# The last two column blocks of an attention output projection, split by token halves

## The chip, the cores and the metric

The kernel runs on one core of a Trainium2 chip. The metric is the device time of one execution in microseconds (us), shown as the median of several runs. A profile of one execution gives, for each engine, when every instruction ran and what ended the idle time in front of it: TensorE (PE, with its weight loads PEld), VectorE (DVE), ScalarE (ACT), GpSimd (POOL) and the queue of DMA issues on SyncE (SP).

## The reference

The reference is a two-layer diffusion backbone over 512 latent tokens of width 2048 with a context of 256 tokens. The part around the change is the end of layer 0 and the start of layer 1:

```
y    = concat(y_a, y_b) * silu(gate)              # 512 x 2048
o    = y @ w_out                                  # w_out: 2048 x 2048
x1   = layer_norm(sqrt(2) * x + g_l * o) * g + bias
h    = layer_norm(x1) * (1 + scale) + shift       # layer 1
u, gate = split(h @ w_in, 2)
f    = real(fft2(u per group of 256 columns))
```

The Fourier step over the tokens is done by the kernel as a product with a 512 x 512 matrix (`dft`) ahead of `h @ w_in`.

## The kernel before

Everything is float32; a product is made of three float32r products of high and low parts (`mm3`: hi*hi, lo*hi, hi*lo). `split` makes the two parts of a tile: a cast on ACT (line 41, `hi`) and a subtraction on DVE (line 44, `lo`).

`out_proj` (called by `mixer_out`) computes `y @ w_out`. The 2048 output columns are four blocks of 512 (`n` = 0 to 3). Within a block, the 16 tiles of the contraction (`k`) come in the order of memory: one DMA brings `raw`, two `k` of 128 x 512 (512 KB), each `k` is split into `pgh` and `pgl`, and for each of the four token tiles of 128 (`t` = 0 to 3) three matmuls of 128x128 by 128x512 add it to that token tile's accumulator `oacc` in PSUM. In this text such a split `k` is a page: it costs 12 matmuls for four token tiles and 6 for two. `raw` has 3 buffers, `pgh` and `pgl` have 7. At the end of a block each token tile gets its epilogue on DVE: `tg` = `oacc` times the gate (line 972; `gate` has one buffer, loaded once per block), `xp` = sqrt(2) * `xr` + `tg` (line 976; `xr` is a block of `x`, two buffers), and its sums (line 977).

Block 3 is done in two groups: all 16 `k` for token tiles 0 and 1, then all 16 `k` again for token tiles 2 and 3, with the same weights loaded and split a second time. After the first group `done(1)` runs the two layer norms of token tiles 0 and 1 while TensorE works for tiles 2 and 3: `centre` (line 1034), `power` and `refine` on POOL (lines 1040 to 1047), `affine` (line 1056) for tile 0, and for tile 1 a scale on ACT (line 1137) and one multiplication and one addition per half, the first half on POOL and the second on DVE (lines 1142 and 1143). The results are stored as `x_0` and `x_1` in four DMAs. `late()`, after the second group's weights, and `done(3)`, after its epilogues, bring the rest, among it the first products with `dft` (`contract`). In the last group the last 6 pages are held back (`hold`): tile 2 gets all six first, then tile 3.

```
self.load(self.x1_d[1][:, cs], x[:, cs], True)     # x_1: a store, issued on SP
```

So loads and these stores go out on one queue, SP's, in the order of the program; a DMA that waits for its source or its buffer holds back what stands behind it.

In blocks 0 to 2 a second stream runs on DVE: `tick()` after each page (in block 0 from `k` = 8) takes one 512 KB tile of the modulation weights of layer 1 (`macraw`, three buffers) and adds it to `mac` in two steps (line 197). Forty ticks in all: 8, 16 and 16.

The order of each engine's instructions is made by a scheduler from the program's order and from the readiness that it estimates; calls with `keep_in_program_order` keep theirs.

Of the kernel before, what the change touches and what calls it, by code (L numbers as in the profile page):

```python
# [10 lines left out]
F32 = mybir.dt.float32  # L11
F32R = mybir.dt.float32r
AF = mybir.ActivationFunctionType
ALU = mybir.AluOpType
# [4 lines left out]
ALPHA = math.sqrt(2.0)  # L19
# [5 lines left out]
class Build:  # L25
# [903 lines left out]

    def out_proj(self, w, nk, y, gate_d, res, xp, rawp, pg, tp, acp, st, kq, hold, done, every, late, first=lambda n: None):  # L930
        nc = self.nc
        for n in range(4):
            first(n)
            gt = tp.tile([128, 512], F32, name="gate", bufs=1)
            self.load(gt, gate_d[n])
            acs = [acp.tile([128, 512], F32, name="oacc") for _ in range(4)]
            groups = [(0, 1, 2, 3)] if n < 3 else [(0, 1), (2, 3)]
            for group in groups:
                end = group[-1] == 3 and n == 3
                held = []  # L940
                for q in range(nk // kq):
                    for kk in range(kq):
                        y(kq * q + kk)
                    raw = rawp.tile([128, kq, 512], F32, name="raw")
                    self.load(raw, w(n, q))
                    for kk in range(kq):
                        k = kq * q + kk
                        yh, yl = y(k)
                        hi = pg.tile([128, 512], F32R, name="pgh")
                        lo = pg.tile([128, 512], F32R, name="pgl")  # L950
                        self.split(raw[:, kk, :], hi, lo)
                        if end and k >= nk - hold:
                            held.append((k, hi, lo))
                            continue
                        for t in group:
                            o = 128 * t
                            self.mm3(acs[t], (yh[:, o:o + 128], yl[:, o:o + 128]), (hi, lo), k == 0, k == nk - 1)
                        if every and n < 3 and (n or k >= 8):
                            self.mac_hold = n == 0
                            self.tick()  # L960
                if n == 3 and not end:
                    self.mac_rest()
                if end:
                    late()
                for t in group:
                    o = 128 * t
                    for k, hi, lo in held:
                        self.mm3(acs[t], (y(k)[0][:, o:o + 128], y(k)[1][:, o:o + 128]), (hi, lo), False, k == nk - 1)
                    xr = tp.tile([128, 512], F32, name="xr")
                    self.load(xr, res(t, n))  # L970
                    g = tp.tile([128, 512], F32, name="tg")
                    ins = nc.vector.tensor_mul(out=g, in0=acs[t], in1=gt)
                    if end and t == 3:
                        self.tc.keep_in_program_order(ins)
                    xs = xp[t][:, 512 * n:512 * n + 512]
                    nc.vector.scalar_tensor_tensor(out=xs, in0=xr, scalar=ALPHA, in1=g, op0=ALU.mult, op1=ALU.add)
                    nc.vector.bn_stats(out=st[t][:, n, :], in_=xs)
                    if n == 3:
                        done(t)

    def mixer_out(self, s):
        nc, d = self.nc, self.d
# [719 lines left out]
```

## Time and profile before

| | us |
|---|---|
| median of 3 runs | 2333.34 (2333.04 to 2336.59) |
| the profiled execution | 2323.94, its span 2322.2 |
| TensorE busy | 2147.6 (92% of the span) |
| output projection, first to last matmul | 939.1 to 1143.2 |

The profiled execution lies 9.4 us (0.4%) under the median of the runs. TensorE is busy in most slices of the span; the stretch from the last block of the output projection to the first products of layer 1 is one of those in which it is not.

### The profile page before, as it was taken

How to read it: one execution, taken by the hardware profiler on the slowest of the kernel's cores; microseconds unless marked ns; L12 is line 12 of the kernel's file. 1: busy time of each engine (PE TensorE's matmuls, PEld its weight loads, DVE VectorE, ACT ScalarE, POOL GpSimd, SP SyncE). 2: the span in 40 equal slices, each digit the busy share in tenths (PEclk: the TensorE clock that was granted, in tenths of full speed). 3: DMA queues.
4: the chain of work that ended last, by engine and by line, in shares of the span. 5: the costliest groups of instructions: out<-in, count | busy, mean ns of one | idle time of the engine just before them, and what ended most of it. 6: DMA issues, size and time to landing. Idle time of an engine off the chain costs nothing.

```text
span 2322.2 us, 39267 instructions
## 1 busy us (share of the span) xinstructions
PE 2147.6 (92%) x15708; PEld 1994.3 (86%) x15708; DVE 1886.4 (81%) x2603; ACT 947.0 (41%) x1321; POOL 429.0 (18%) x407
## 2 busy tenths in 40 slices
PE   5999989989999999999788999998999998998994
PEld 3778879889899999777568989998999998998994
DVE  5456799998765588677799998789899899779998
ACT  2222344433444467322463333444343445445331
POOL 1023413100111123000551131002122124002003
PEclk9999999999999999999999999999999999999997
DMA  8852354566511132787427765545455446537333
GB/s 339 310 196 95 124 183 159 188 230 208 208 48 58 60 110 75 229 300 261 169 96 252 273 242 181 182 146 188 156 175 193 150 166 230 174 128 255 117 137 118
DMA packets 128702, 412.63 MB, mean 178 GB/s; under 512 B 14852, under 2 KB 15492, under 8 KB 126728
## 3 DMA queue, kind: packets, MB, share of 16 engines
q1 hardware_dynamic: 113144, 359.04, 45.3%
q0 software_dynamic: 8320, 31.33, 3.8%
q10 hardware_dynamic: 7056, 19.76, 2.2%
q8 instruction: 123, 2.02, 0.4%
q14 instruction: 59, 0.48, 0.1%
HBM read 347.81 MB, written 62.26 MB: 177 GB/s over the span
## 4 chain that ended last, share of the span: by engine, by line
PE 35%; DVE 8%; DMA 3%; issue 3%; ACT 1%; POOL 1%; DVEq 0%; SPq 0%; ACTq 0%; POOLq 0%
PE r L54 33%; DVE wl L44 2%; DMA wraw<-in_wg 2%; PE psd L54 1%; DVE mac L197 1%; DMA stage<-yt 1%; DVE wraw L1185 1%; DVE btl L44 1%; DVE ws L1206 0%; DVE x L1539 0%; DVE c L1219 0%; PE pt L1492 0%; DVE hf L1325 0%; DVE x L1535 0%; POOL btl L44 0%
## 5 line engine op out<-in xcount | busy, mean ns | idle before, releaser
L54 PE MATMUL r<-bth,wl 128*128 128x256 f32 x1848 | 525.1, 284 | 16.8 <-DVE wl L44 16.5
L54 PE MATMUL r<-btl,wh 128*128 128x256 f32 x1848 | 524.6, 284 | 2.3 <-DVE btl L44 1.3
L54 PE MATMUL r<-bth,wh 128*128 128x256 f32 x1848 | 525.2, 284 | 0.2 <-ACT wh L41 0.2
L41 ACT CAST wh<-wraw 128x1024 fp32r<-128x1024 f32 x262 | 274.6, 1050 | 393.1 <-PE r L54 288.0
L44 DVE TENSOR_TENSOR wl<-wraw,wh 128x1024 fp32r<-128x1024 f32 x262 | 335.0, 1283 | 52.3 <-ACT wh L41 52.0
L54 PEld LDWEIGHTS r<-bth,wl 128*128 128x128 f32 x1848 | 351.4, 190 | 19.5 <-DVE wl L44 19.2
L54 PEld LDWEIGHTS r<-btl,wh 128*128 128x128 f32 x1848 | 350.8, 190 | 3.6 <-DVE btl L44 1.7
L54 PEld LDWEIGHTS r<-bth,wh 128*128 128x128 f32 x1848 | 351.8, 190 | 0.9 <-issue 0.5
L41 ACT CAST wh<-ws 128x1024 fp32r<-128x1024 f32 x183 | 191.8, 1049 | 344.3 <-PE r L54 330.4
L44 DVE TENSOR_TENSOR wl<-ws,wh 128x1024 fp32r<-128x1024 f32 x183 | 230.0, 1257 | 12.0 <-ACT wh L41 9.8
L197 DVE SCALAR_TENSOR_TENSOR mac<-macraw,cs,mac 128x512 f32<-128x512 f32 x240 | 193.6, 807 | 11.4 <-DMA macraw<-in_ada 9.9
L54 PE MATMUL r<-hlh,wl 128*128 128x256 f32 (+1 forms) x480 | 147.2, 307 | 26.7 <-DVE wl L44 26.6
L54 PE MATMUL r<-hlh,wh 128*128 128x256 f32 (+1 forms) x480 | 146.3, 305 | 0.6 <-ACT wh L41 0.5
L54 PE MATMUL r<-hll,wh 128*128 128x256 f32 (+1 forms) x480 | 144.9, 302 | 0.0
L54 PE MATMUL r<-bah,wl 128*128 128x256 f32 x384 | 112.7, 293 | 25.1 <-DVE wl L44 25.1
L54 PEld LDWEIGHTS r<-hlh,wl 128*128 128x128 f32 x480 | 93.5, 195 | 33.7 <-DVE wl L44 30.7
L41 ACT CAST pgh<-raw 128x512 fp32r<-128x512 f32 (+2 forms) x104 | 65.7, 662 | 121.8 <-DMA raw<-in_wo 78.2
L54 PE MATMUL r<-bbh,wl 128*128 128x256 f32 x384 | 109.5, 285 | 2.9 <-DVE wl L44 2.9
L54 PE MATMUL r<-bal,wh 128*128 128x256 f32 x384 | 111.2, 290 | 0.0
L54 PE MATMUL oacc<-pgl,yh 128*128 128x512 f32 x256 | 102.1, 399 | 9.7 <-DVE pgl L44 9.7
L54 PE MATMUL r<-bah,wh 128*128 128x256 f32 x384 | 111.1, 289 | 0.0
L54 PE MATMUL r<-bbh,wh 128*128 128x256 f32 x384 | 109.4, 285 | 0.0
(489 smaller groups left out, 5700.1 us busy)
## 6 DMA issues: line engine op xcount, KB each, us to landing
macraw<-in_ada SPq DMA_DIRECT2D x72, 512.0 KB, 6.3
wraw<-in_win SPq DMA_DIRECT2D x66, 512.0 KB, 6.7
raw<-in_adas SPq DMA_DIRECT2D x64, 512.0 KB, 5.1
wraw<-in_wg SPq DMA_DIRECT2D x64, 512.0 KB, 6.6
wraw<-in_wu SPq DMA_DIRECT2D x64, 512.0 KB, 4.3
wraw<-in_wo SPq DMA_DIRECT2D x64, 512.0 KB, 4.7
macraw<-in_ada SPq DMA_DIRECT2D x112, 256.0 KB, 3.9
raw<-in_wo SPq DMA_DIRECT2D x40, 512.0 KB, 5.4
```

Source lines behind the costliest of these rows:

```text
L41: ins = nc.scalar.copy(out=hi, in_=src)
L44: sub = (eng or nc.vector).tensor_sub(out=lo, in0=src, in1=hi.bitcast(F32))
L54: self.pin(self.nc.tensor.matmul(ps, lhsT=a, rhs=b, start=start, stop=stop))
L197: ins = nc.vector.scalar_tensor_tensor(out=acc, in0=raw[:, k, :], scalar=col, in1=acc, op0=ALU.mult, op1=ALU.add)
L1185: nc.vector.tensor_sub(out=raw[1, 0], in0=raw[0, 0], in1=raw[1, 0])
```

## The change

The list of blocks and groups is written out: blocks 0 and 1 for all token tiles, then blocks 2 and 3 for tiles 0 and 1, then blocks 2 and 3 for tiles 2 and 3. In this text the four groups are (2,01), (3,01), (2,23) and (3,23). The weights of block 2 are now loaded and split twice, as those of block 3 were, and the gate of blocks 2 and 3 is loaded for each group. The sixteen ticks of block 2 all stay with its first group. The matmuls are the same in number.

```diff
-        for n in range(4):
-            first(n)
+        every4 = (0, 1, 2, 3)
+        for n, group in ((0, every4), (1, every4), (2, (0, 1)), (3, (0, 1)), (2, (2, 3)), (3, (2, 3))):
+            if group[0] == 0:
+                first(n)
             gt = tp.tile([128, 512], F32, name="gate", bufs=1)
             self.load(gt, gate_d[n])
-            acs = [acp.tile([128, 512], F32, name="oacc") for _ in range(4)]
-            groups = [(0, 1, 2, 3)] if n < 3 else [(0, 1), (2, 3)]
-            for group in groups:
-                end = group[-1] == 3 and n == 3
+            acs = {t: acp.tile([128, 512], F32, name="oacc") for t in group}
+            end = group[-1] == 3 and n == 3
...
-                        if every and n < 3 and (n or k >= 8):
+                    if every and n < 3 and group[0] == 0 and (n or k >= 8):
...
```

The rest of the diff is one level of indentation.

On SP, the queue from the loads of (3,01) on stands so before (`raw`, `gate` and `xr` are loads, `x_0` to `x_3` the stores of the normalized tokens):

```order
L62 DMA gate<-gate_3_97 128x512
L62 DMA xr<-in_x 128x512 x2
L62 DMA raw<-in_wo 128x1024 x8
L62 DMA xr<-in_x 128x512 x2
L62 DMA raw<-in_wo 128x1024 x2
L62 DMA x_0_10166<-xp 128x1024 x2
L62 DMA x_1_10167<-xp 128x1024 x2
L62 DMA x_3_10169<-lngb 128x1024 x2
```

And so from the same place in the changed kernel:

```order
L62 DMA raw<-in_wo 128x1024 x11
L62 DMA gate<-gate_2_96 128x512
L62 DMA xr<-in_x 128x512 x2
L62 DMA raw<-in_wo 128x1024 x2
L62 DMA x_0_10166<-xp 128x1024 x2
L62 DMA x_1_10167<-xp 128x1024 x2
L62 DMA raw<-in_wo 128x1024 x3
L62 DMA gate<-gate_3_97 128x512
L62 DMA xr<-in_x 128x512 x2
L62 DMA raw<-in_wo 128x1024 x5
L62 DMA x_3_10169<-lngb 128x1024 x2
```

Before, no weight load stands behind the four stores; now all eight of (3,23) do (3 and 5).

On DVE, from the last two `pgl` of block 2 to the first of block 3, before:

```order
L44 TENSOR_TENSOR pgl<-raw,pgh 128x512 x2
L197 SCALAR_TENSOR_TENSOR mac<-macraw,cs,mac 128x512 x4
L44 TENSOR_TENSOR pgl<-raw,pgh 128x512 x6
L972 TENSOR_TENSOR tg<-oacc,gate 128x512 x2
L976 SCALAR_TENSOR_TENSOR xp<-xr,tg 128x512 x2
```

And in the changed kernel:

```order
L44 TENSOR_TENSOR pgl<-raw,pgh 128x512 x2
L197 SCALAR_TENSOR_TENSOR mac<-macraw,cs,mac 128x512 x2
L972 TENSOR_TENSOR tg<-oacc,gate 128x512
L197 SCALAR_TENSOR_TENSOR mac<-macraw,cs,mac 128x512
L976 SCALAR_TENSOR_TENSOR xp<-xr,tg 128x512
L197 SCALAR_TENSOR_TENSOR mac<-macraw,cs,mac 128x512
L977 BN_STATS st_10162<-xp 128x6
L972 TENSOR_TENSOR tg<-oacc,gate 128x512
L44 TENSOR_TENSOR pgl<-raw,pgh 128x512
```

The first `tg` (which waits for block 2's last page) now stands ahead of block 3's first `pgl` instead of six behind it.

On DVE at the end of (2,23) in the changed kernel, from the last step of the norm of tile 1:

```order
L1143 TENSOR_TENSOR xp<-xp,lnbb 128x1024
L44 TENSOR_TENSOR pgl<-raw,pgh 128x512 x6
L972 TENSOR_TENSOR tg<-oacc,gate 128x512 x2
L976 SCALAR_TENSOR_TENSOR xp<-xr,tg 128x512 x2
L977 BN_STATS st_10164<-xp 128x6
L977 BN_STATS st_10165<-xp 128x6
L44 TENSOR_TENSOR pgl<-raw,pgh 128x512 x15
```

Of the six `pgl`, five are the last of (2,23) and one is the first of (3,23); the six epilogue instructions of (2,23) stand between (3,23)'s first `pgl` and its other fifteen. Up to this place the order of DVE after (3,01) is as it was before, with four `pgl` where six stand now.

## Rows read from the trace of the kernel before

**Rows 1.** Windows: us, busy PE, PEld, DVE, ACT, POOL, then clock, DMA share, GB/s

```profile
1050.20:1090.00 39.80, 39.79 (x179) 33.05 (x180) 32.41 (x51) 9.14 (x16) 0.00 (x0) 1.00 0.81 270
...
1114.20:1143.20 29.00, 24.07 (x94) 18.14 (x93) 26.50 (x36) 12.82 (x18) 16.36 (x18) 0.94 0.44 153
1143.20:1167.00 23.80, 11.90 (x42) 7.93 (x40) 15.10 (x28) 12.18 (x19) 15.52 (x15) 0.86 0.40 139
```

**Rows 2.** Timeline of PE: start, us, instruction, [idle before, releaser]; 60 matmuls apart

```profile
1054.69 0.39 PE L54 MATMUL oacc<-pgh,yl 128*128 128x512 f32 x1
...
1068.29 0.39 PE L54 MATMUL oacc<-pgh,yl 128*128 128x512 f32 x1
```

**Rows 3.** Lines of DVE by shape in 1049.4 to 1083: count, busy, mean, idle before

```profile
L197 DVE SCALAR_TENSOR_TENSOR mac<-macraw,cs,mac 128x512 f32<-128x512 f32 x25 | 18.7, 750 | 3.9 <-DMA macraw<-in_ada 3.4
L44 DVE TENSOR_TENSOR pgl<-raw,pgh 128x512 fp32r<-128x512 f32 x14 | 9.4, 687 | 2.6 <-ACT pgh L41 2.5
```

**Rows 4.** Timeline of DVE: block 2's last `pgl`, then its first epilogues

```profile
1080.08 1.29 DVE L44 TENSOR_TENSOR pgl<-raw,pgh 128x512 fp32r<-128x512 f32 x2 [0.37 <-ACT pgh L41]
1081.29 3.11 DVE L197 SCALAR_TENSOR_TENSOR mac<-macraw,cs,mac 128x512 f32<-128x512 f32 x4
...
1088.93 1.28 DVE L972 TENSOR_TENSOR tg<-oacc,gate 128x512 f32<-128x512 f32 x2
1090.13 1.28 DVE L976 SCALAR_TENSOR_TENSOR xp<-xr,tg 128x512 f32<-128x512 f32 x2
```

**Rows 5.** Timeline of PE: two waits and the matmuls behind the first

```profile
993.22 1.87 PE L219 MATMUL oacc<-ones,mac 128*128 128x1 f32 x8 [5.05 <-DVE tg L972]
...
995.52 0.63 PE L54 MATMUL oacc<-pgl,yh 128*128 128x512 f32 x1
...
1000.22 0.63 PE L54 MATMUL oacc<-pgh,yh 128*128 128x512 f32 x1
...
1050.21 0.50 PE L54 MATMUL oacc<-pgl,yh 128*128 128x512 f32 x1 [3.19 <-DVE pgl L44]
```

**Rows 6.** Timeline of DVE after (3,01): its first `tg`, the last four `pgl`

```profile
1114.24 0.69 DVE L972 TENSOR_TENSOR tg<-oacc,gate 128x512 f32<-128x512 f32 x1
...
1130.29 6.83 DVE L44 TENSOR_TENSOR pgl<-raw,pgh 128x512 fp32r<-128x512 f32 x4
```

**Rows 7.** Timeline of PE: its last waits of the projection, a slow matmul, the last

```profile
1134.42 0.51 PE L54 MATMUL oacc<-pgl,yh 128*128 128x512 f32 x1 [1.74 <-DVE pgl L44]
...
1137.18 0.70 PE L54 MATMUL oacc<-pgl,yh 128*128 128x512 f32 x1 [1.79 <-DVE pgl L44]
...
1138.54 0.63 PE L54 MATMUL oacc<-pgh,yh 128*128 128x512 f32 x1
...
1142.78 0.39 PE L54 MATMUL oacc<-pgh,yl 128*128 128x512 f32 x1
```

**Rows 8.** Timeline of POOL: the last step of tile 1's first half

```profile
1133.89 2.69 POOL L1143 TENSOR_TENSOR xp<-xp,lnbb 128x1024 f32<-128x1024 f32 x1
```

**Rows 9.** Timeline of SP: the four stores

```profile
1126.33 11.07 SPq L62 DMA_DIRECT2D x<-xp  x4
```

**Rows 10.** Waits of SP in 1040 to 1143: total us, times, longest

```profile
SPq L62 <- POOL xp L1143: 8.7, 1, 8.7
```

**Rows 11.** Tile `raw` in 1040 to 1143: casts, idle ahead of them, landing

```profile
L41 ACT CAST pgh<-raw x46: 602/619/624, 1040.6 to 1131.4; 128x512 fp32r<-128x512 f32 x46
...
  DMA raw<-in_wo: 48.9, 12
...
DMA to landing us min/median/max: 3.5/5.1/7.8
```

**Rows 12.** Timeline of DVE behind the last matmul: token tile 3

```profile
1143.93 1.47 DVE L976 SCALAR_TENSOR_TENSOR xp<-xr,tg 128x512 f32<-128x512 f32 x1
```

**Rows 13.** Timeline of POOL at the same time: token tile 0

```profile
1142.90 1.96 POOL L1087 TENSOR_TENSOR macraw<-xp,macraw 128x768 fp32r<-128x768 f32 x1 [3.08 <-ACT macraw L1086]
```

**Rows 14.** Timeline of ACT behind the projection

```profile
1155.55 1.24 ACT L1076 ACTIVATE xp<-xp,smx 128x1024 f32<-128x1024 f32 x1 [8.41 <-POOL smx L1071]
```

More of the change, by code (lines that the diff above doesn't have):

```diff
@@ L931, in out_proj @@
         nc = self.nc
-        for n in range(4):
-            first(n)
+        every4 = (0, 1, 2, 3)
+        for n, group in ((0, every4), (1, every4), (2, (0, 1)), (3, (0, 1)), (2, (2, 3)), (3, (2, 3))):
+            if group[0] == 0:
+                first(n)
             gt = tp.tile([128, 512], F32, name="gate", bufs=1)
             self.load(gt, gate_d[n])
-            acs = [acp.tile([128, 512], F32, name="oacc") for _ in range(4)]
-            groups = [(0, 1, 2, 3)] if n < 3 else [(0, 1), (2, 3)]
-            for group in groups:
-                end = group[-1] == 3 and n == 3
[L940 to L957, printed above, removed]
-                        if every and n < 3 and (n or k >= 8):
[L959 to L979, printed above, removed]
@@ new lines, in out_proj @@
+            acs = {t: acp.tile([128, 512], F32, name="oacc") for t in group}
+            end = group[-1] == 3 and n == 3
+            held = []
+            for q in range(nk // kq):
+                for kk in range(kq):
+                    y(kq * q + kk)
+                raw = rawp.tile([128, kq, 512], F32, name="raw")
+                self.load(raw, w(n, q))
+                for kk in range(kq):
+                    k = kq * q + kk
+                    yh, yl = y(k)
+                    hi = pg.tile([128, 512], F32R, name="pgh")
+                    lo = pg.tile([128, 512], F32R, name="pgl")
+                    self.split(raw[:, kk, :], hi, lo)
+                    if end and k >= nk - hold:
+                        held.append((k, hi, lo))
+                        continue
+                    for t in group:
+                        o = 128 * t
+                        self.mm3(acs[t], (yh[:, o:o + 128], yl[:, o:o + 128]), (hi, lo), k == 0, k == nk - 1)
+                    if every and n < 3 and group[0] == 0 and (n or k >= 8):
+                        self.mac_hold = n == 0
+                        self.tick()
@@ new lines, in out_proj @@
+            if n == 3 and not end:
+                self.mac_rest()
+            if end:
+                late()
+            for t in group:
+                o = 128 * t
+                for k, hi, lo in held:
+                    self.mm3(acs[t], (y(k)[0][:, o:o + 128], y(k)[1][:, o:o + 128]), (hi, lo), False, k == nk - 1)
+                xr = tp.tile([128, 512], F32, name="xr")
+                self.load(xr, res(t, n))
+                g = tp.tile([128, 512], F32, name="tg")
+                ins = nc.vector.tensor_mul(out=g, in0=acs[t], in1=gt)
+                if end and t == 3:
+                    self.tc.keep_in_program_order(ins)
+                xs = xp[t][:, 512 * n:512 * n + 512]
+                nc.vector.scalar_tensor_tensor(out=xs, in0=xr, scalar=ALPHA, in1=g, op0=ALU.mult, op1=ALU.add)
+                nc.vector.bn_stats(out=st[t][:, n, :], in_=xs)
+                if n == 3:
+                    done(t)
```

## The prediction

> **What bounds the kernel now.** I read the windows first: they tell stage by stage which engine is full. From 1050 to 1090, block 2, TensorE is busy without a break (39.79 of 39.80 us at clock 1.00), but DVE is busy for 32.41 us of it and the DMA engines for 81%: TensorE is the bound with little room beside it. From 1114.2 to 1143.2, the second group of block 3, TensorE loses 5 us and part of its clock, and in the 24 us behind it, where the last norms run, it is busy for half [rows 1]. So a change here can gain in the last two windows and has little slack to spend in the first.
>
> Next the timeline of TensorE, for the price of a page. Sixty matmuls take 1068.29 - 1054.69 = 13.60 us, 0.2267 us each [rows 2]: a page costs 12 x 0.2267 = 2.72 us for four token tiles and 1.36 us for two. A group of two tiles is 16 pages, 21.8 us.
>
> Then DVE in block 2. Fourteen of its sixteen `pgl` and 25 of the tick's additions take 9.4 + 18.7 us in 33 us, and of DVE's 6.5 us of waits 3.4 name `macraw`'s DMA and 2.5 a cast [rows 3], and what ACT waits for ahead of casts is the load of `raw`, 48.9 us in this stretch [rows 11]. Little of that waits for TensorE. Block 2 needs those instructions whether a page feeds 12 matmuls or 6.
>
> Last the queue of SP, whose four stores take from 1126.33 to 1137.40 to be issued [rows 9]; 8.7 us of that is one wait for POOL's last step on tile 1 [rows 10], which ends at 1133.89 + 2.69 = 1136.58 [rows 8]. Today nothing that TensorE needs stands behind these stores.
>
> **The change part by part.** The matmuls stay 768. Added are 16 casts and 16 `pgl`, 8 loads of 512 KB and 2 of a gate. I walk along TensorE's path with the mark M, the start of DVE's first `tg` after (3,01): 1114.24 before [rows 6]. The last matmul then starts at 1142.78 and the group ends at 1143.0 [rows 7], M + 28.8.
>
> *Group (2,01).* DVE's instructions up to block 2's last `pgl` are the same ones in nearly the same order, and so is SP's queue; what they waited for was not TensorE. So that `pgl` again ends at 1080.08 + 1.29 = 1081.4 [rows 4]. But TensorE, which then had 7.5 us of matmuls in hand (to the `tg` at 1088.93), now has only the last two pages, about 10 matmuls from 1080.7 on: it finishes at 1083.0 at full clock, or at 1085.0 at the lower one (0.427 us each, from (1000.22 - 995.52) / 11 in [rows 5]), which its waits in this group may bring. From 1050.21 on [rows 5] it has done 14 pages, 19.0 us, in 33 to 35: some 15 us idle. The first `tg` starts 0.5 to 0.7 us ahead of that end, 1082.5 to 1084.3. Behind it on DVE stand mac, STT, mac, BN, `tg`, and only then block 3's first `pgl`: seven instructions, five at 0.60 (pairs start 1.20 apart) and two at 0.78 (four in 3.11) [rows 4], 4.5 us. TensorE waits about 4 us and goes on at 1087.0 to 1088.8.
>
> *Group (3,01).* 94 matmuls are left, 21.3 us. Its first six pages come from loads issued before the epilogue; the next `raw` follows the second `xr`, about 1.3 us behind that first `pgl`, and with a landing of 5.1 [rows 11], a cast and a `pgl` page 6 is ready 7.6 us behind it, just when it is due (6 x 1.36 less two matmuls is 7.7): no wait, and none to spare. Whether the clock falls in the 4 us wait is open: after 5.05 us of idling it was low for 12 matmuls and more (0.63 long against 0.39), after 3.19 us it was not [rows 5]. A fall costs 13 x 0.2 = 2.6 us; this wait lies between the two, I take half. M comes at 1107.6 to 1112.0, middle 1109.8: **-4.4** (-6.6 to -2.2).
>
> *Group (2,23).* It stands where (3,23) stood, against the same norms of tiles 0 and 1 on DVE, ACT and POOL. The last `pgl` was ready at 1137.18 [rows 7], M + 22.9 (the four `pgl` before it had taken 6.83 us beside POOL [rows 6, 8]); four matmuls later, at M + 23.8, the group ends. The waits of 1.74 and 1.79 us that the change might have spared stay, in this group.
>
> *Group (3,23): the new wait.* Its eight loads stand behind the four stores. The last store is issued at 1137.40, M + 23.2 [rows 9]. A `raw` lands 3.5 to 7.8 us after issue, median 5.1 [rows 11]; the other queues being quiet then (DMA share of the window 0.44 [rows 1]) I take 4.0, bounds 3.5 and 5.1. With 0.6 for the cast [rows 11] TensorE starts at M + 27.8: a wait of **4.0**. The first `pgl` ends at M + 28.4; behind it DVE has six epilogue instructions of (2,23), held there by that `pgl`, 3.6 us at the starts of [rows 4], and then the second `pgl`, ready at M + 32.6. TensorE's first page is done at M + 29.3: a second wait of **3.3**. From there 88 matmuls, 19.95 us, to M + 52.6. The gate and the fourth `raw` follow the epilogues and land about when page 6 is due, so they add nothing I can price. The clock fell before after two waits of 1.74 and 1.79 us close together [rows 7]; with 4.0 and 3.3 I take the fall, 2.6 us. End at **M + 55.2** (52.1 to 56.3), against M + 28.8.
>
> *Behind the projection.* The norms of tiles 2 and 3 start from the last matmuls as before, in the same order on DVE, ACT and POOL; ACT still waits there for POOL's root of tile 1 [rows 14], which stands behind tile 3's own statistics. Only tile 0's last step on POOL, which ran against tile 3's `xp` [rows 13] and drew it to 1.47 us where 0.69 is usual [rows 6, 12], is now done earlier: **-0.8**.
>
> Sum: -4.4 + 55.2 - 28.8 - 0.8 = **+21 us**, between -6.6 + 52.1 - 28.8 - 0.8 = +16 and -2.2 + 56.3 - 28.8 - 0.8 = +24.5. The profiled execution would take 2323.9 + 21 = 2345, the median of the runs, which lies 9.4 us above it, 2333.3 + 21 = **2354 us**.
>
> The Trainium skill, "TensorE: Matmul & The Clock Gate", Part 1, has the array run at 1.2 GHz by default and at 2.4 GHz only after sustained activity, so that each long idle stretch is paid twice. The trace agrees for the idle stretch of 5.05 us and not for the one of 3.19 [rows 5]. With the rule taken for every new wait the sum would be +23.4, with no fall at all +16.4.
>
> **The rivals.**
>
> *No wait at the queue.* The stores get ready early enough, or the loads come from elsewhere, and (3,23) follows (2,23) at once: without 4.0, 3.3 and the fall of the clock, 9.9 us, +11, 2344.5. Against it: POOL's half of tile 1 ended at M + 22.3 [rows 8] and nothing in the change makes it faster. It decides from a store issued at M + 19.2, 4 us sooner, on.
>
> *The tick stream spreads.* If the 6.5 us of waits in (2,01) shrink as well, since TensorE no longer holds page buffers, and the queue does not wait, +11 - 6.5 = +4.5, about no change. Against it: those waits name DMAs [rows 3].
>
> *Faster: the doubled group hides everything.* If (2,01) ran at TensorE's pace, the added work lay under the other groups, and tiles 0 and 1 were normalized so early that the projection's end lost its waits, the gain would be what the window from 1114.2 shows: 29.00 - 24.07 = 4.9 us of idle [rows 1] and some 8 slow matmuls at 0.2 behind 1137.18 [rows 7], 6.5 us in all, 2327. It decides whether DVE can do its 28 us of `pgl` and additions of (2,01) [rows 3] within TensorE's 21.8; the row says no, even without waits.
>
> *Worse.* The DMA engines are 81% busy in block 2 [rows 1], and a `raw` can take 7.8 us to land [rows 11]. Where the first one of (3,23) does, 2.7 us are added to the upper end, and as much again where the fourth does: +27 to +30, 2360 to 2363.
>
> **How the numbers follow.** The forecast (+16 to +24.5) gets 0.74, no wait at the queue 0.10, worse 0.08, about no change 0.03, faster 0.05. The forecast's own range is 2349 to 2358; for 8 in 10, with room for the first rival and part of the worse case, I give 2343 to 2361. About 0.2% (4.7 us) is what a measurement of this kernel can tell from no change. Slower by more than that: 0.74 + 0.10 + 0.08 = 0.92; within it 0.03; faster 0.05.
>
> **What the changed profile would show.** TensorE idle for some 15 us within (2,01), waiting for `pgl`, with DVE and DMA as full as before; about 4 us between (2,01) and (3,01) with `tg` on DVE ahead of the `pgl`; the first `tg` after (3,01) within 7 us ahead of 1114; then (2,23) with waits like those of (3,23) before; SP's first `raw` of (3,23) right behind the store that waits for POOL; two waits of TensorE around 4 and 3 us; the last matmul of the projection 20 to 25 us later; and the same 24 us behind it. The prediction is wrong if (2,01) takes TensorE's time and not DVE's, if those loads are issued before POOL is done, or if the norms behind the projection get shorter by more than a microsecond.

## The result and the profile after

The changed kernel takes 2352.1 us (median of 4 runs) against 2333.2 of the kernel before on the same chip: ratio 1.009 (95% interval 1.0074 to 1.0107). A second comparison on another chip gave 1.0103 (1.0086 to 1.0119), 2355.8 against 2331.3 us. So it is slower, by 18.9 and 24.5 us where 21 was forecast.

Executions of one kernel differ by several us, and most of that arises long before the change: block 1's first `tg` on DVE came 1040.7 to 1051.2 us into the span in fourteen profiles, though the kernels are the same, or nearly, up to there. I therefore read each profile from that `tg` on (1040.70 in the profile of before) to the `tg` of token tile 3, and call this the stretch. It took 102.5 us before (1143.20 - 1040.70) and 127.65 after (below): +25.15. A second pair of profiles gave 103.87 and 129.03: +25.16.

The windows after, which answer to [rows 1]: the four groups, and the norms behind them (us, busy PE, PEld, DVE, ACT, POOL, granted clock, DMA share, GB/s).

```profile
1050.20:1085.00 34.80, 26.44 (x91) 20.23 (x92) 27.77 (x46) 7.28 (x14) 0.00 (x0) 0.79 0.86 289
1085.00:1110.00 25.00, 23.64 (x99) 18.97 (x98) 16.73 (x29) 11.02 (x20) 0.00 (x0) 0.92 0.63 207
1110.00:1134.00 24.00, 23.55 (x104) 18.84 (x102) 18.53 (x30) 10.61 (x16) 14.33 (x9) 1.00 0.53 184
1134.00:1163.00 29.00, 19.71 (x77) 15.06 (x76) 13.73 (x22) 10.04 (x17) 2.45 (x9) 0.82 0.64 209
1163.00:1187.00 24.00, 14.17 (x54) 10.67 (x53) 15.65 (x23) 12.37 (x17) 13.31 (x12) 0.74 0.30 109
```

Two groups lose: the first, (2,01), and the last, (3,23). TensorE's waits, which answer to [rows 5, 7], say what each waited for:

```profile
1050.96 0.79 PE L54 MATMUL oacc<-pgl,yh 128*128 128x512 f32 x1 [6.93 <-DVE pgl L44]
1064.30 0.73 PE L54 MATMUL oacc<-pgh,yh 128*128 128x512 f32 x2 [0.73 <-ACT pgh L41]
1072.42 1.22 PE L54 MATMUL oacc<-pgh,yh 128*128 128x512 f32 x2 [4.10 <-ACT pgh L41]
1079.64 1.22 PE L54 MATMUL oacc<-pgh,yh 128*128 128x512 f32 x2 [2.77 <-ACT pgh L41]
1086.56 1.05 PE L219 MATMUL oacc<-ones,mac 128*128 128x1 f32 x8 [0.62 <-DVE mac L197]
1088.35 0.50 PE L54 MATMUL oacc<-pgl,yh 128*128 128x512 f32 x1 [0.74 <-DVE pgl L44]
1125.78 0.50 PE L54 MATMUL oacc<-pgl,yh 128*128 128x512 f32 x1 [0.36 <-DVE pgl L44]
1142.84 0.80 PE L54 MATMUL oacc<-pgh,yh 128*128 128x512 f32 x1 [8.46 <-ACT pgh L41]
1147.76 0.51 PE L54 MATMUL oacc<-pgl,yh 128*128 128x512 f32 x1 [0.83 <-DVE pgl L44]
```

6.93 + 0.73 + 4.10 + 2.77 = 14.5 us are idle at the start of (2,01) and in it (3.19 us of such a wait stood at the start of block 2 before, [rows 5]), and 8.46 us ahead of (3,23). The landmarks on DVE, which answer to [rows 4, 6]:

```profile
1041.54 1.28 DVE L972 TENSOR_TENSOR tg<-oacc,gate 128x512 f32<-128x512 f32 x2
...
1079.62 1.29 DVE L44 TENSOR_TENSOR pgl<-raw,pgh 128x512 fp32r<-128x512 f32 x2 [0.42 <-ACT pgh L41]
...
1083.89 0.69 DVE L972 TENSOR_TENSOR tg<-oacc,gate 128x512 f32<-128x512 f32 x1 [1.52 <-PE oacc L54]
...
1111.54 1.28 DVE L972 TENSOR_TENSOR tg<-oacc,gate 128x512 f32<-128x512 f32 x2
...
1126.79 3.08 DVE L44 TENSOR_TENSOR pgl<-raw,pgh 128x512 fp32r<-128x512 f32 x5
...
1169.19 0.68 DVE L972 TENSOR_TENSOR tg<-oacc,gate 128x512 f32<-128x512 f32 x1
```

And the queue on SP, POOL's steps on tile 1 and ACT's first cast of (3,23), which answer to [rows 8 to 10]:

```profile
1122.82 12.60 SPq L62 DMA_DIRECT2D x<-xp  x4
1135.51 2.48 SPq L62 DMA_DIRECT2D raw<-in_wo  x3
...
1123.75 8.39 POOL L1142 TENSOR_TENSOR xp<-xp,lngb 128x1024 f32<-128x1024 f32 x1 [2.22 <-ACT xp L1137]
1132.21 2.38 POOL L1143 TENSOR_TENSOR xp<-xp,lnbb 128x1024 f32<-128x1024 f32 x1
...
1142.17 3.69 ACT L41 CAST pgh<-raw 128x512 fp32r<-128x512 f32 x6 [13.65 <-DMA raw<-in_wo]
```

The first load of (3,23) is issued at 1135.51, right behind the last store, which waited for POOL's step to end at 1134.59 (1132.21 + 2.38), and ACT has had nothing to cast for 13.65 us when the load lands.

### The profile page after: what moved, and what is told of

Its sections match the earlier page's. It is cut to its first block, busy times and chain, and to the rows that moved or that the text cites. A ratio compares the mean times of both kernels' runs of the same rounds, so it can differ in the third digit from the quotient of the medians.

```text
span 2349.0 us, 39335 instructions
## 1 busy us (share of the span) xinstructions
PE 2156.1 (92%) x15708; PEld 1999.8 (85%) x15708; DVE 1892.7 (81%) x2619; ACT 956.1 (41%) x1337; POOL 431.2 (18%) x407
## 4 chain that ended last, share of the span: by engine, by line
PE 34%; DVE 8%; issue 3%; DMA 3%; ACT 1%; POOL 1%; DVEq 0%; SPq 0%; ACTq 0%; POOLq 0%
PE r L54 33%; DVE wl L44 2%; DMA wraw<-in_wg 2%; PE psd L54 1%; DVE mac L197 1%; DVE wraw L1185 1%; DVE btl L44 0%; DVE ws L1206 0%; DMA stage<-yt 0%; DVE x L1539 0%; DMA wraw<-in_wu 0%; DVE c L1219 0%; POOL btl L44 0%; PE pt L1492 0%; DVE hf L1325 0%
## 5 line engine op out<-in xcount | busy, mean ns | idle before, releaser
L41 ACT CAST wh<-wraw 128x1024 fp32r<-128x1024 f32 x262 | 274.6, 1050 | 397.5 <-PE r L54 282.4
L41 ACT CAST pgh<-raw 128x512 fp32r<-128x512 f32 (+2 forms) x120 | 74.8, 656 | 143.2 <-DMA raw<-in_wo 101.6
L44 DVE TENSOR_TENSOR pgl<-raw,pgh 128x512 fp32r<-128x512 f32 (+2 forms) x120 | 85.9, 738 | 49.4 <-ACT pgh L41 49.2
L54 PE MATMUL oacc<-pgh,yh 128*128 128x512 f32 x256 | 104.7, 416 | 18.4 <-ACT pgh L41 16.1
```

The source lines that it names most:

```text
L41: ins = nc.scalar.copy(out=hi, in_=src)
L44: sub = (eng or nc.vector).tensor_sub(out=lo, in0=src, in1=hi.bitcast(F32))
L54: self.pin(self.nc.tensor.matmul(ps, lhsT=a, rhs=b, start=start, stop=stop))
```

## The experiments

All distances are from block 1's first `tg`, read from DVE's timeline of each profile.

| | first `tg` of (2,01) | of (3,01) | of (2,23) | tile 3, end | ratio to before (95%) |
|---|---|---|---|---|---|
| before | | 73.5 | | 102.5 | |
| before again | | 73.8 | | 103.9 | 0.9997 (0.9987 to 1.0007) |
| changed | 42.4 | 70.0 | 101.9 | 127.7 | 1.0090 (1.0074 to 1.0107) |
| changed again | 42.2 | 69.2 | 100.9 | 129.0 | 1.0103 (1.0086 to 1.0119) |
| stores last | 41.7 | 69.1 | 94.2 | 116.3 | 1.0082 (1.0067 to 1.0097) |
| small stores | 43.2 | 70.7 | 103.0 | 126.8 | 1.0114 (1.0093 to 1.0135) |
| ticks spread | 26.0 | 54.4 | 96.9 | 119.8 | 1.0080 (1.0061 to 1.0098) |
| block 2 alone | 43.0 | 92.3 | 72.0 | 124.6 | 1.0121 (1.0101 to 1.0141) |
| both repairs | 27.9 | 56.6 | 90.0 | 111.1 | 1.0040 (1.0024 to 1.0056) |
| both, norm early | 28.4 | 58.1 | 92.0 | 112.7 | 1.0011 (0.9998 to 1.0023) |
| light adds | 42.7 | 68.6 | 97.7 | 126.2 | 1.0096 (1.0076 to 1.0116) |
| light loads | 32.6 | 63.9 | 92.1 | 119.9 | 1.0069 (1.0050 to 1.0089) |
| before, norm early | | 72.4 | | 102.2 | 0.9988 (0.9970 to 1.0006) |
| four groups | 27.2 | 52.4 | 83.7 | 108.8 | 1.0016 (0.9999 to 1.0033) |

My theory was the prediction's: (2,01) is paced by the tick stream, and (3,23) waits for loads that stand behind the stores. The rivals: the waits at (3,23) come from DVE and POOL themselves; the loads of the weights alone pace (2,01).

**Stores last.** The first line stood in `done(1)`.

```diff
-                        self.load(self.x1_d[1][:, cs], x[:, cs], True)
...
             def late():
                 x = self.xp[1]
+                for cs in halves:
+                    self.load(self.x1_d[1][:, cs], x[:, cs], True)
```

> The two stores of tile 1 (x_1) stand behind the eight loads of (3,23) instead of ahead of them; all else is as in the changed kernel. If the loads waited for their place in the queue (the theory), the first raw of (3,23) is issued some 10 us sooner, TensorE's waits of 8.46 and 0.83 us at the start of (3,23) and about 3 us of slow clock behind them go, and the time falls by 9.9 to 12.5 us from the changed kernel's 2352: 2340 to 2342, ratio to the kernel before 1.003 to 1.004. If those waits come from DVE and POOL, which still work on tile 1 then, the loads land early and TensorE waits for pgl as long as before: 2350 to 2353.

SP's queue, and TensorE's only two waits from the end of (3,01) to the last matmul of the projection:

```profile
1129.02 1.52 SPq L62 DMA_DIRECT2D x<-xp  x2
1133.69 9.61 SPq L62 DMA_DIRECT2D raw<-in_wo  x5
...
1150.93 1.07 SPq L62 DMA_DIRECT2D x<-xp  x2
...
1131.98 0.50 PE L54 MATMUL oacc<-pgl,yh 128*128 128x512 f32 x1 [1.75 <-DVE pgl L44]
1147.18 0.50 PE L54 MATMUL oacc<-pgl,yh 128*128 128x512 f32 x1 [0.90 <-DVE pgl L44]
```

The wait of 8.46 us is gone, and the stretch is 11.3 us shorter. The rival falls: DVE and POOL did the same work, POOL's step at its 8.4 us again. But the 9.9 to 12.5 us were expected of the time, and the time missed them: 2346.0 us and a ratio of 1.0082, between the two cases and not clear of the changed kernel's 1.0090 and 1.0103. This profile's span is 6.4 us under that of the first changed one, with block 1 beginning 7.1 us later (1048.64); it is the fastest of its five runs, so that start may not be this execution's alone, and where it comes from is open. I go by the stretch here; the ratio shows the same edit below, in both repairs.

**Small stores.** The edit above, and in the old place:

```diff
+                        self.load(self.x1_d[1][:, cs.start:cs.start + 16], x[:, cs.start:cs.start + 16], True)
```

> In the place of the two stores of tile 1 stand two stores of 16 columns each (8 KB), which wait for the same steps of POOL and DVE; the whole tile is stored again behind the loads of (3,23). So the wait in the queue is left and the megabyte that went ahead of the loads is taken out. If only the wait for POOL counts, TensorE still waits about 8.5 us ahead of (3,23) and the time is that of the changed kernel, 2351 to 2353. If the store's bytes also held up the loads (1 MB at the 400 GB/s that the rows show there is 2.6 us; the first load landed 6.6 us after issue where 4.0 was reckoned), that wait is 5.5 to 6.5 us and the time 2348 to 2350.

Queue, cast and TensorE:

```profile
1129.12 12.60 SPq L62 DMA_DIRECT2D x<-xp  x4
1141.81 8.76 SPq L62 DMA_DIRECT2D raw<-in_wo  x5
...
1146.80 1.14 ACT L41 CAST pgh<-raw 128x512 fp32r<-128x512 f32 x2 [11.98 <-DMA raw<-in_wo]
...
1147.47 0.79 PE L54 MATMUL oacc<-pgh,yh 128*128 128x512 f32 x1 [6.79 <-ACT pgh L41]
```

The place in the queue costs most: the stores still take 12.60 us. TensorE's wait, 6.79 us, lies between the two cases and nearer the second. The first cast starts 4.99 us behind the load's issue where it was 6.66 (1142.17 - 1135.51; 6.50 in the second profile of the changed kernel, and 3.88 with the stores last), so a megabyte of stores ahead on the same queue cost some 1.6 us more. The stretch won 0.9 us of it, and the time, 2353.3 us, is that of the first case.

**Ticks spread.**

```diff
-                    if every and n < 3 and group[0] == 0 and (n or k >= 8):
+                    if every and group[0] == 0 and (n or k >= 8) and (n < 2 or k % 2 == 0):
```

> The sixteen ticks of block 2 go eight to (2,01) and eight to (3,01), one after every second page; all else is as in the changed kernel. If (2,01) was paced by the tick stream (the theory), each of the two groups now has some 11 us of pgl and 12 of additions on DVE and about 8.4 MB to load in 21.8 us: TensorE's idle time from 1050 to the end of (3,01) falls from 16.6 us to 3 to 7, some slow clock goes with it, and the time falls by 10 to 15 us: 2337 to 2342. If the loads of weights alone set the pace of (2,01), or DVE is only moved into (3,01), the idle time turns up there and the time is 2347 to 2353.

The end of (3,01) comes 15.6 us sooner (54.4 against 70.0), and TensorE's waits from 1050 to there sum to 5.9 us, as expected, so it is not the weights alone that pace (2,01). But the same wait in the queue met TensorE earlier still, inside (2,23):

```profile
1132.67 1.22 PE L54 MATMUL oacc<-pgh,yh 128*128 128x512 f32 x2 [8.99 <-ACT pgh L41]
```

(2,23) took 42.5 us from `tg` to `tg`, and 7.8 of the 15.6 us are left at the end. The time, 2344.9 us, falls between the two cases.

**Both repairs** together.

> Both repairs at once: x_1 stored behind the loads of (3,23), and the ticks of block 2 spread over (2,01) and (3,01). Alone, the first shortened the stretch by 11.3 us (127.6 to 116.3), and the second brought the end of (3,01) 15.6 us nearer (from 70.0 to 54.4 us behind block 1's first tg) but lost half of it again to longer waits for loads behind the stores. If those two causes are all of the loss, they add up: a stretch of 100 to 102 us, about that of the kernel before, ratio 0.998 to 1.001. If DVE and POOL, with the norms of tiles 0 and 1, are the next limit, the stretch is 104 to 110 and the ratio 1.001 to 1.004.

They don't add up to the kernel before: 111.1, the second case, a little over its range. Against ticks spread, from which this version differs by the stores alone, the stretch is 8.7 us shorter and the ratio falls from 1.0080 to 1.0040, some 9 us, with intervals that don't meet: so the cost of the queue shows in the whole time too. From 1072 to 1100 DMA is still busy for 86%, and (2,23) takes 33.4 us, with waits for `pgl` beside the norms of tiles 0 and 1 (3.44 and 2.37 us the longest).

**Block 2 alone.**

```diff
-        for n, group in ((0, every4), (1, every4), (2, (0, 1)), (3, (0, 1)), (2, (2, 3)), (3, (2, 3))):
+        for n, group in ((0, every4), (1, every4), (2, (0, 1)), (2, (2, 3)), (3, (0, 1)), (3, (2, 3))):
```

> The same four groups in the order (2,01), (2,23), (3,01), (3,23): block 2 is split, and the end is that of the kernel before, with no load of weights behind the stores. By the theory the loss of (2,01) is left (about 15 us of idle time and 2 to 4 of slow clock, some 18 of the 26 us by which the end of the projection moved in the profiles) and what the queue cost is gone (8.5 + 0.8 + about 3): 2338 to 2342, so 10 to 14 less than the changed kernel. If (2,23), free of ticks, lets the loads run ahead and gives back part of the loss, it is nearer to the kernel before, 2333 to 2338. If the order doesn't matter, it is as the changed kernel, 2350 to 2353.

A miss: the stretch is 3.0 us shorter than the changed kernel's, not 10 to 14, and the ratio shows not even that. The end of (3,01) comes 18.7 us later than before, as the theory has it; but the last group, with no queue to wait for, took 32.3 us where it took 29.0 before. POOL, DVE and TensorE there:

```profile
1152.49 2.50 POOL L1142 TENSOR_TENSOR xp<-xp,lngb 128x1024 f32<-128x1024 f32 x1 [2.22 <-ACT xp L1137]
...
1152.65 3.42 DVE L1142 TENSOR_TENSOR xp<-xp,lngb 128x1024 f32<-128x1024 f32 x1
1156.00 2.83 DVE L44 TENSOR_TENSOR pgl<-raw,pgh 128x512 fp32r<-128x512 f32 x1
...
1158.88 0.80 PE L54 MATMUL oacc<-pgl,yh 128*128 128x512 f32 x1 [4.13 <-DVE pgl L44]
```

Here POOL's multiplication takes 2.50 us and not 8.39, and DVE's, 1.21 otherwise, and its next `pgl` take 3.42 and 2.83. TensorE waits 4.13 us at once. So the group beside the norms costs 3 to 4 us in waits, in the kernel before too (1.74 + 1.79, [rows 7]). In the changed kernel it was spared most of them (0.36, and 1.33 in the second profile), with a slower POOL; stores last had 1.75 with the same slow POOL.

**Before and changed again**, to see what differs from execution to execution.

> The kernel before, unchanged, as a measure of what differs from execution to execution. The stretch from the first tg of block 1 to the tg of token tile 3 took 102.5 us in its first profile, and it should take 102 to 103 again; the start of that stretch, 1040.7 in the first profile and 1046.6 to 1048.6 in the profiles of the four changed versions, should be late here too if the difference lies in the execution and not in the kernels. Ratio 0.999 to 1.001.

> The changed kernel, unchanged, on the chip of the others. The stretch from block 1's first tg to the tg of token tile 3 should take 127 to 128.5 us as in its first profile. If the 25 us by which that stretch is longer than before are all there is, the ratio is about 1.0105 to 1.011; if the runs give back part of it elsewhere, it is again 1.009 or less.

Both stretches came out 1.4 us longer than the first time, just over what was expected, their difference the same; the ratio of the second, 1.0103, lies between its two cases. The start of before's moved by 2.4 us only. A late start needs no split, since the unsplit kernel with the norm early, below, began at 1051.15; but I can't say whether all the later starts lie in the executions alone. Nor do stretch and time agree everywhere: the changed kernel's first 25.2 us show as 18.9 in the time, the 13.8 of stores last (116.3 - 102.5) as 18.2.

**Light adds** and **light loads**: which half of the tick stream paces (2,01)?

```diff
+                    m = 128 if len(chunks) == 5 and n >= 24 else 512
-                    ins = nc.vector.scalar_tensor_tensor(out=acc, in0=raw[:, k, :], scalar=col, in1=acc,
+                    ins = nc.vector.scalar_tensor_tensor(out=acc[:, 0:m], in0=raw[:, k, 0:m], scalar=col, in1=acc[:, 0:m],
```

```diff
-        self.load(raw, src[chunk if layer else chunk - 8, q, :, o], True)
+        m = 128 if self.light and self.light.pop(0) else 512
+        self.load(raw[:, :, 0:m], src[chunk if layer else chunk - 8, q, :, o][:, :, 0:m], True)
...
+                    rv = raw[:, k, None, 0:128].broadcast_to([128, 4, 128])
...
```

The first edit leaves three quarters of the columns out of the additions, the second out of the loads; the last line shown has DVE read the loaded quarter four times over.

> The changed kernel with the additions of block 2's sixteen ticks on 128 of 512 columns (the rest of two rows of modulation is left out); their loads are whole. It tells DVE's share in the pace of (2,01) from that of the loads. In both profiles of the changed kernel its first tg comes 42.3 us behind block 1's first. DVE's 16 pgl (11 us) and 32 additions (24 us) with the seven epilogues of block 1 ahead of them make 42. If DVE alone sets the pace, the distance falls to TensorE's, 25 to 28 us (26.0 with half of the ticks). If the loads alone do (12.6 MB at the 290 to 310 GB/s that the windows show is 41 us, less what is loaded ahead), it stays at 37 to 42. If both do, it falls little here and little with light loads.

> The other half: block 2's sixteen ticks load 128 of 512 columns (128 KB each in place of 512) and DVE adds these four times over, so that its instructions keep their size (two rows of modulation come out other than they should). 6.3 MB are left to load in (2,01), 21 us at 300 GB/s. If the loads alone set the pace, the first tg of (2,01) comes 25 to 28 us behind block 1's first instead of 42.3. If DVE does, it stays at 39 to 42.

DVE's lines by shape in (2,01), light adds first (1052 to 1084), then light loads (1058 to 1084):

```profile
L44 DVE TENSOR_TENSOR pgl<-raw,pgh 128x512 fp32r<-128x512 f32 x14 | 9.2, 686 | 4.6 <-ACT pgh L41 4.5
L198 DVE SCALAR_TENSOR_TENSOR mac<-macraw,cs,mac 128x128 f32<-128x128 f32 x24 | 8.4, 350 | 6.5 <-DMA macraw<-in_ada 6.0
```

```profile
L207 DVE SCALAR_TENSOR_TENSOR mac<-macraw,cs,mac 128x512 f32<-128x512 f32 x20 | 14.6, 744 | 0.0
L44 DVE TENSOR_TENSOR pgl<-raw,pgh 128x512 fp32r<-128x512 f32 x14 | 9.6, 683 | 0.4 <-ACT pgh L41 0.4
```

With additions of 350 ns instead of 749, (2,01) ends no sooner (42.7): what DVE saves it waits for DMA (6.0) and for casts (4.5). With a quarter of the bytes it ends 9.8 us sooner (32.6), and now DVE waits for nothing (0.0 and 0.4) and is full. So the loads set the pace, and DVE comes next, 10 us below: neither case as I had put it, but nearer to the loads. What holds the loads themselves is only in part known. (2,01) needs 12.6 MB, which at 359 GB/s, the fullest 10 us read here (ticks spread, 1040 to 1050), would take 35 us, an estimate: TensorE's 21.8 were out of reach. But it moved 289 GB/s, and for 20.3 of the 35 us from 1050 to 1085 SP's queue waited for DVE's additions to free a `macraw` buffer. Whether more buffers or a second queue would bring it nearer to 35 was not tried.

**Norm early**: a way that both kernels could go, because ACT waits behind the projection for POOL's root of tile 1, 8.4 and 8.7 us before [rows 14] and 11.5 and 13.1 in the changed kernel. This is the edit to the kernel before; `root` and `normal` of tile 1 go from `done(3)`. With both repairs the two `normal` of tile 1 stay there.

```diff
             def late():
                 x = self.xp[1]
-                normal(nc.scalar, 0, self.xp[0], slice(0, 2048))
-                soon(0)
                 hold(nc.scalar.activation(out=junk, in_=x, func=AF.Copy, scale=-1.0 / 2048, accum_out=sm[:, 1, 1:2]))
                 for h in range(2):
                     square(1, x, h)
+                root(nc.gpsimd, 1, 2)
+                normal(nc.scalar, 0, self.xp[0], slice(0, 2048))
+                normal(nc.gpsimd, 1, x, halves[0])
+                soon(0)
+                normal(nc.scalar, 1, x, halves[1])
...
```

> As the version with both repairs, and the inverse deviation of tile 1's second norm (eight small steps on POOL) is worked out as soon as tile 1 is stored, ahead of tile 3's statistics and not behind them; ACT takes the sums of tile 1 ahead of the last step on tile 0. Before, ACT waits 8.4 us there for POOL and then squares tile 3 about 5.5 us later than it could. If that wait lies on the path, the transposes behind it come 4 to 5 us sooner after the tg of tile 3 (22.5 us in the first profile of before, 17.5 to 18.5 here), and the ratio is 0.002 below that of the version with both repairs. If another engine is the next to wait for, the distance stays at 21 to 23.

> The kernel before, without the change, with tile 1's second norm worked out as soon as tile 1 is stored: the sums on ACT ahead of the last step on tile 0, the deviation and the normalizing ahead of tile 3's statistics. ACT then has no wait of 8.4 to 8.7 us behind the squares of tile 1, and the squares of tiles 3 and 2 follow DVE's steps. If that wait lies on the path, tile 3's transposes come 18 to 19.5 us behind its tg instead of 21.8, and with the rest of the projection as before the ratio is 0.998 to 0.999, the only version here that beats the kernel before. If POOL's work then holds up DVE's steps on tiles 2 and 3, the distance stays at 21 to 23 and the ratio at 1.000.

In the kernel before, tile 3's transposes come 20.1 us behind its `tg` instead of 21.8, and with both repairs 19.7: some 2 us, not 4 to 5. ACT's wait shrinks to 2.25, but POOL's work now falls on DVE's steps for tiles 3 and 2 (2.34 and 2.48 before):

```profile
1155.39 1.24 ACT L1076 ACTIVATE xp<-xp,smx 128x1024 f32<-128x1024 f32 x1 [2.25 <-POOL smx L1071]
...
1156.47 3.99 DVE L1034 SCALAR_TENSOR_TENSOR xp<-xp,mvs,lngb 128x2048 f32<-128x2048 f32 x1
...
1164.56 4.02 DVE L1056 SCALAR_TENSOR_TENSOR xp<-xp,smx,lnbb 128x1024 f32<-128x1024 f32 x2
```

The ratio, 0.9988, has an interval that reaches over 1: not shown faster. With both repairs the ratio falls by 0.0029, some 7 us, more than these 2; the profiles don't show where the rest comes from.

**Four groups**: is there a form of the split that gains? This version has stores last and the norm early as well; the edit shows the ticks.

```diff
-                    if every and n < 3 and group[0] == 0 and (n or k >= 8):
+                    if every and (n < 2 and (n or k >= 8) or k in ticks.get((n, group[0]), ())):
...
+        ticks = {(2, 0): (0, 3, 6, 9, 12), (3, 0): (0, 4, 8, 12), (2, 2): (0, 5, 10), (3, 2): (0, 2, 4, 6)}
...
```

> The split kernel with x_1 stored behind the loads of (3,23), tile 1's second norm early as in the kernel before with that edit, and block 2's ticks spread over all four groups (5, 4, 3 and 4). The loads decide: the four groups have 16.8 MB of weights and 8.4 MB of modulation to bring in 87 us of matmuls, 290 GB/s, as much as (2,01) got while it waited for them. If the loads are all there is to it, evenly spread they just keep up: the stretch from block 1's first tg to the tg of token tile 3 is 100 to 104 us (102.5 and 103.9 in the kernel before) and the ratio 0.997 to 1.000. If the norms of tiles 0 and 1 on DVE and POOL hold up (2,23) as in the version with both repairs (33.4 us from tg to tg there, 21.8 on TensorE alone), the stretch is 106 to 112 and the ratio 1.001 to 1.004, and the split has no form here that gains.

The loads keep up through (3,01) (52.4), but (2,23) takes 31.4 us beside the norms: POOL's step takes 2.45 and DVE's 3.37 + 2.83, as in the version with block 2 alone, and TensorE waits 6.69 us for one `pgl`. 108.8 us: the second case. No form of the split tried here is shown faster than the kernel before.

## Why the prediction came out as it did

The direction and the two places of the loss were right. Of the sum, +21 (16 to 24.5), -0.8 lay behind the stretch, so it stood for +22 in the stretch, which shows +25.2. The 3.1 us more are 0.9 in M, 1.1 at the end of (3,23), where two errors nearly cancel, and 1.1 behind it, which the sum did not have: DVE's `tg` of tile 3 stands behind its steps on tile 2 and starts 1.3 us after TensorE's end (0.2 before). Step by step:

*(2,01)* was right in time. The last `pgl` ends at 1080.9 (1081.4 said), the first `tg` starts at 1083.89 (1082.5 to 1084.3), TensorE goes on at 1088.35 (1087.0 to 1088.8). The 15 us that TensorE was to lose from 1050.21 on came, but as 8.4 us of idling (34.80 - 26.44 in the first window) and some 6 of low clock (0.79 there): 91 matmuls were busy for 26.4 us, where 0.2267 each would be 20.6. The wait of about 4 behind it shows as 0.62 + 0.74, since slow matmuls and `ones` fill the rest. The reason was half right: I had DVE's additions decide, and light adds against light loads show that the loads do, with DVE next.

*(3,01)*: M at 1111.54, -2.7 where -4.4 stood; with block 1's `tg` 0.84 later in this execution, -3.5, and -4.6 in the second pair of profiles. The clock did fall, for the eight matmuls from 1089.2 to 1092.5 (granted clock 0.92 in that window), some 1.6 us, where I had taken half of a fall, 1.3 of 2.6 us; in the second profile it did not fall here.

*(2,23)*: "the waits of 1.74 and 1.79 us stay" failed. They became one of 0.36 (1.33 in the second profile), and TensorE was done at 1142.84 - 8.46 = 1134.38, M + 22.8 and not 23.8, because DVE's `pgl` went on at 0.6 us apiece (five in 3.08) where four had taken 6.83 [rows 6], and POOL's multiplication took 8.39 for 6.56.

*(3,23)*: the term was 4.0 + 3.3 + 2.6 = 9.9, and taking the stores out of the queue gave back 10.4 between M and the end (127.65 - 70.00 against 116.32 - 69.10). Inside it the first wait was too small, 8.46 for 4.0: 1.0 because (2,23) ended sooner, 0.8 because POOL released the store later (issue at M + 24.0, not 23.2), 2.7 because the load took 6.66 us to the cast and not 4.0. Small stores give some 1.6 of that to the store's own bytes. The second wait shows as 0.83, but from one start of TensorE to the next, 4.92 us, it is the 4.8 that was reckoned. The fall of the clock, 2.6, cost almost nothing in this profile: the slow matmuls of the first page ran while TensorE would have waited for that second `pgl`, and from 1147.76 to the last one's start at 1167.64 the matmuls took 19.9 us, 88 at the 0.2267 of full clock. In the second profile the clock stayed low for ten more matmuls behind the second wait, and the same 88 took 21.97 us:

```profile
1148.10 0.80 PE L54 MATMUL oacc<-pgl,yh 128*128 128x512 f32 x1 [0.83 <-DVE pgl L44]
...
1152.11 0.63 PE L54 MATMUL oacc<-pgh,yl 128*128 128x512 f32 x1
...
1170.07 0.39 PE L54 MATMUL oacc<-pgh,yl 128*128 128x512 f32 x1
```

So the fall cost 2.1 us there, close to the 2.6 reckoned. That (3,23) ended at M + 56.3 in the first profile, at the upper bound, is in part luck: a first wait 4.5 too small against a fall that cost nothing. In the second it ended at M + 58.3, beyond the bound.

*Behind the projection*: the transposes came at 22.55 us after tile 3's `tg` before and at 21.77 after, -0.8 as said, but for another reason: in the second profile of before they came at 21.78 too. The slow `xp` of 1.47 us [rows 12] was one of a single execution (0.69 in the second), and the change has no share in it.

The Trainium skill, "TensorE: Matmul & The Clock Gate", Part 1, taken for every new wait, gave +23.4. The rows agree in part: the clock was low behind the wait ahead of (3,23) in both profiles of the changed kernel, behind the one ahead of (3,01) in the first alone, and where a second wait covered the slow matmuls, the fall cost nothing.

Of the rivals, "no wait at the queue" and "the tick stream spreads" are what the two repairs made of the kernel, and "worse" came nearest: the load did land late, by 2.7 us.

## What to carry to other kernels

Splitting an output block by rows halves the matmuls behind each loaded and split weight, so reckon the loads, the splits and every stream that shares the stage against half the matmul time, the loads first: here 12.6 MB had to come in 22 us, and (2,01) ended 42 us behind block 1's first `tg`. Look along the issue queue for a transfer that waits for a slow engine: everything behind it waits too, and it is cheap to move. And price a single execution's odd row (1.47 where 0.69 is usual) at nothing until a second profile shows it again.

## What the runs showed of the hardware

When POOL multiplies 1024 columns beside DVE, POOL starts 0.16 to 0.17 us ahead of DVE's half in all fourteen profiles, and yet there are three outcomes, each the same to 0.05 us wherever it comes: POOL 6.56 and DVE's next four `pgl` 6.83 instead of some 2.5 (the two profiles of the kernel before and its variant); POOL 8.38 and DVE as if alone, 1.21 and 0.68 (seven profiles, both of the changed kernel among them); POOL 2.45 to 2.50 and DVE 3.37 to 3.42 and 2.83 (four). The Trainium skill, "SBUF — State Buffer", "Who interferes with whom", says that the two engines share a port pair, that one blocks the other fully for an instruction, and that the order of issue decides which. The runs agree that one holds up the other (in the last four, DVE's 2.2 us more are about POOL's 2.50). That the order decides they don't bear out, as far as the starts in the profiles tell: it was the same in all, and in ten of them POOL, the first to start, took far longer than 2.5 us. What does decide is open, and no experiment here tried it. TensorE's longest wait for a `pgl` in that group lay between 0.36 us (POOL at 8.39) and 6.69 (POOL at 2.45); the versions differ in more than this, so its own price is not shown.
